# The second expert rows of token block 0 are fetched in the front, by halves

## The chip, the cores and the metric

One NeuronCore of a Trainium2 chip runs the whole program in one launch. The figure of merit is the device time in microseconds. The kernel before takes 3671.69 us, the median of 3 runs (3661.53 to 3674.93). The engines are PE (TensorE, matrix multiply), DVE (VectorE), ACT (ScalarE), POOL (GpSimd, which issues the gathers by index) and SP (SyncE, which issues the plain loads and stores).

## The reference, cut to what matters

There are 1024 tokens of 1024 features, in 8 blocks of 128 tokens. A mixing part (latent attention with rotary positions, a gated linear recurrence, a merge) gives `h2`. Then comes an expert layer, in float32:

```python
s = einsum('thpd,hpnd->thpn', (xt @ w_query).reshape(...), sub_keys)   # 8 heads, 2 halves, 128 keys
s_top, i_top = top_k(s, 16); best, pos = top_k(cand, 16)               # 16 of 16384 experts per head
u = expert_u[idx]; v = expert_v[idx]                                   # 128 rows of 1024 per token, each
act = gelu(einsum('td,thkd->thk', xt, u))
x  += gate2 * einsum('thk,thkd->td', softmax(best) * act, v)
```

So each token needs 128 "first rows" of `expert_u` (dot products) and 128 "second rows" of `expert_v` (a weighted sum). Both tables hold 16384 rows of 4 KB, 67 MB each.

## The kernel before

**Front.** The tokens go through the mixing part in two halves of 512 (p = 0 and p = 1): attention, the gate of branch A with its projection (`merge_a`), the recurrence (`lru`), the gate of branch B with its projection (`merge_b`), the output projection (`ffn_in`, tiles `ps_z`) and the expert query (`ps_qr`, `ps_sc`) with its top 16. A float32 product is made of three passes over a high and a low part (lines 686, 687, 689).

**Last stage (`dense`, from about 1656 us).** Blocks 1, 2, 3 and 4 are not gathered. PE goes through all 128 groups of 128 experts: it multiplies the group's `expert_u` with these 512 tokens (`ps_A`, 24 matmuls), weighs the result with a table of chosen experts (`Gt`, read from `d_G`) and multiplies with the group's `expert_v` (`ps_y`, 96 matmuls for each four groups). Both tables are read once, in order, by SP (`raw<-in_uT`, `raw<-in_expert_v`), 512 KB each.

**Gathered blocks.** Blocks 0, 5, 6 and 7 fetch their rows by index. For the first rows POOL issues one indirect DMA for each of the 128 choices: 128 tokens, 4 KB each (`g_u`), and DVE makes the dot product (lines 1120 and 1140). For the second rows POOL fetches, token by token, that token's 128 rows (`g_v`, line 1160), and PE sums them: the weights stand in one column of a zero tile of 32 columns, four tokens side by side in the four column groups of PE (`g_y`, line 1174, two passes for each float32 product). The expert numbers are `ei`, their transpose `eT`, the weights `wT`.

**What sets the order.** Beside the main program there is a list of small steps. `pump(n)` takes the next n steps from it at many places of the main program; `self.rate` says how many (attention unit, weight matrix `w`, `z`, `q`). In the second half of the front the list holds block 0's first rows, three choices a step through three buffers (43 steps), spread evenly (`merge`) among the steps that build the tables of the dense blocks 1 to 3 (`differ`, `keys`, `product`, `leave`: tiles `ps_d`, `oneA`, `oneB`, `ps_G`, `gs`). What is left is done before the last stage begins. In `dense` the list is paced evenly: `points = (128 + 32*4) * RATE` (248 with `RATE` 0.97) and `rate = len(steps) / points`, one point for each 24 matmuls. Before, that list has 959 steps: 131 gathers of first rows each for blocks 5, 6, 7 and 128 of second rows each for blocks 0, 5, 6, 7, with some steps around them, and the routing of 6 and 7. The two kinds are merged with each other:

```python
self.steps += self.merge(us[5][:48], routes) + self.merge(us[5][48:], vs[0][:80]) + \
    self.merge(us[6], vs[0][80:] + vs[5][:64]) + self.merge(us[7], vs[5][64:] + vs[6][:64]) + \
    vs[6][64:] + vs[7]
```

A scheduler then sets the order on each engine; each engine takes its instructions in that order, and one that waits holds up all behind it. Front tiles come from pools in SBUF (tags `t2`, `t4`, `gu`, ...) and from 8 PSUM banks (`ps`).

Of the kernel before, what the change touches and what calls it, by code (L numbers as in the profile page):

```python
# [9 lines left out]
F32 = mybir.dt.float32  # L10
F32R = mybir.dt.float32r
I32 = mybir.dt.int32
# [19 lines left out]
GUF = 3  # L32
# [52 lines left out]
class Builder:  # L85
    def __init__(self, ctx, tc, I, out, dbg=None, stop=None):
# [8 lines left out]
        self.rate = dict(unit=(1, 1.6), w=(1.5, 2.2), z=(4, 5), q=(2, 2.5))  # L95
# [149 lines left out]
    def prep(self, ap):  # L245
# [34 lines left out]
        nc.sync.dma_start(gr[:, 1, :], I["k_norm_g"][None, 64:96].to_broadcast([128, 32]))  # L280
        for w in range(2):
            g1 = gr[:, w, None, 0:16].to_broadcast([128, 8, 16])
            g2 = gr[:, w, None, 16:32].to_broadcast([128, 8, 16])
            nc.vector.tensor_tensor(self.tab[:, 2 * w, :, 0:16], cn, g1, op=ALU.mult)
            nc.vector.tensor_tensor(self.tab[:, 2 * w, :, 16:32], sn, g2, op=ALU.mult)
            nc.vector.tensor_tensor(self.tab[:, 2 * w + 1, :, 0:16], sn, g1, op=ALU.mult)
            nc.vector.tensor_tensor(self.tab[:, 2 * w + 1, :, 16:32], cn, g2, op=ALU.mult)
# [91 lines left out]
    def head(self, p):  # L379
# [6 lines left out]
        def load():  # L386
            s["x"] = []
            for i in range(4):
# [277 lines left out]
    def rope(self, dst, src, which, tb, n):  # L666

        nc = self.nc
        t1 = self.tab[:, 2 * which, tb, None, :].rearrange("p o (a b) -> p o a b", a=2).to_broadcast([128, n, 2, 16])
        t2 = self.tab[:, 2 * which + 1, tb, None, :].rearrange("p o (a b) -> p o a b", a=2).to_broadcast([128, n, 2, 16])  # L670
# [286 lines left out]
    def route(self, tb):  # L957
# [83 lines left out]
        def end():  # L1041
# [6 lines left out]
            if tb in GATHER:  # L1048
# [4 lines left out]
                g["eT"] = self.kept(g, [128, 128], I32, "eT")  # L1053
# [8 lines left out]
        def turn():  # L1062
# [3 lines left out]
            nc.vector.tensor_copy(g["eT"], pt)  # L1066
# [8 lines left out]
    def kept(self, g, shape, dt, name):  # L1075

        tb = g["tb"]
        return self.cp.tile(shape, dt, name=f"{name}{tb}") if tb in SOONER or name == "eT" and tb == BRIDGE else \
# [6 lines left out]
    def after_part(self, p):  # L1085
# [5 lines left out]
        if p == 0:  # L1091
            self.steps += rt[0] + self.merge(self.gather_u(self.blocks[0]), dense)
# [55 lines left out]
    def gather_v(self, g):  # L1148
# [30 lines left out]
        return [lambda n=n: step(n) for n in range(128 + GV - 4)] + [lambda: self.finish(gp, g["tb"], g.pop("y"), "gv", GV)]  # L1179

# [206 lines left out]
    def run(self):  # L1387
# [5 lines left out]
        self.d_hT = [dr.tile([128, 4, 512], F32, name=f"d_hT{j}") for j in range(4)]  # L1393
        self.d_v = dr.tile([128, 4, 512], F32, name="d_v")
# [6 lines left out]
        with (tc.tile_pool(name="front_b", bufs=1, reuse_waits="tile") as fb,  # L1401
              tc.tile_pool(name="front_a", bufs=9, reuse_waits="tile") as fa,
              tc.tile_pool(name="ps", bufs=8, space=bass.MemoryType.PSUM, reuse_waits="tile") as self.ps):
            self.fp = Pair(fa, fb, ("b8", "whl", "raw"))
            self.tab = self.fp.tile([128, 4, 8, 32], F32, tag="tab", bufs=1, name="tab")
# [77 lines left out]
```

## Time and profile before

| | |
|---|---|
| median of 3 runs | 3671.69 us |
| the profiled execution | 3655.58 us |
| its span, first to last instruction | 3653.8 us |
| front (to the first `ps_A` matmul) | about 1656 us |
| last stage | about 1998 us |
| PE, DVE, POOL, ACT busy | 87%, 63%, 34%, 33% of the span |
| DMA | 915 MB moved, 250 GB/s over the span |

The profile is one execution. Busy time of an engine says how long instructions ran on it; a wait is idle time before an instruction, put down to what released it. `PEclk` is the clock that PE was granted, as a share of the full 2.4 GHz. The DMA share is the mean busy share of the 16 DMA engines.

### The profile page before, as it was taken

How to read it: one execution, taken by the hardware profiler on the slowest of the kernel's cores; microseconds unless marked ns; L12 is line 12 of the kernel's file. 1: busy time of each engine (PE TensorE's matmuls, PEld its weight loads, DVE VectorE, ACT ScalarE, POOL GpSimd, SP SyncE). 2: the span in 40 equal slices, each digit the busy share in tenths (PEclk: the TensorE clock that was granted, in tenths of full speed). 3: DMA queues.
4: the chain of work that ended last, by engine and by line, in shares of the span. 5: the costliest groups of instructions: out<-in, count | busy, mean ns of one | idle time of the engine just before them, and what ended most of it. 6: DMA issues, size and time to landing. Idle time of an engine off the chain costs nothing.

```text
span 3653.8 us, 42970 instructions
## 1 busy us (share of the span) xinstructions
PE 3189.4 (87%) x15408; PEld 2341.4 (64%) x15408; DVE 2305.6 (63%) x5350; ACT 1189.6 (33%) x1861; POOL 1243.4 (34%) x1052
## 2 busy tenths in 40 slices
PE   6899989599987988867798988898988989899997
PEld 4477778467765776645565665665666666666665
DVE  5535557988788567696965655665646665633334
ACT  4437444376356333233221121121211221212121
POOL 0000013133332000002456645554746655544451
PEclk8899999799998999878999999998999999999999
DMA  8422444166866433228899989898989999999995
GB/s 313 151 85 88 136 152 146 51 200 223 289 209 209 144 116 120 72 110 268 266 338 354 369 309 332 329 346 289 372 307 348 367 338 345 335 345 338 356 362 192
DMA packets 388990, 915.13 MB, mean 250 GB/s; under 512 B 160020, under 2 KB 178068, under 8 KB 384936
## 3 DMA queue, kind: packets, MB, share of 16 engines
q0 software_dynamic: 147456, 536.94, 39.9%
q1 hardware_dynamic: 241320, 375.45, 31.2%
q8 instruction: 121, 1.98, 0.2%
q14 instruction: 93, 0.76, 0.1%
HBM read 851.44 MB, written 60.83 MB: 250 GB/s over the span
## 4 chain that ended last, share of the span: by engine, by line
PE 29%; DMA 28%; DVE 21%; issue 14%; ACT 5%; POOL 3%; SPq 0%; POOLq 0%; DVEq 0%; ACTq 0%
DMA raw<-in_uT 13%; DMA raw<-in_expert_v 6%; DMA g_u<-in_expert_u,g_ei 5%; DVE g_u L1120 3%; PE g_y L1174 2%; DMA g_u<-in_expert_u,ei 2%; PE ps_y L686 2%; DVE v L105 2%; PE ps_G L1238 2%; PE ps_y L687 2%; DVE yac L1347 1%; PE ps_y L689 1%; POOL g_u L1132 1%; DVE u L105 1%; ACT u L104 1%
## 5 line engine op out<-in xcount | busy, mean ns | idle before, releaser
L1120 DVE CUSTOM_DVE_ANT_0 g_u<-g_u,g_h 128x1024 f32<-128x1024 f32 x384 | 462.2, 1220 | 140.8 <-DMA g_u<-in_expert_u,g_ei 81.1
L686 PE MATMUL ps_A<-dh,u 128*128 128x512 f32 x1024 | 443.3, 433 | 117.5 <-ACT u L104 100.9
L686 PE MATMUL ps_y<-v,w 128*128 128x512 f32 x1024 | 419.0, 409 | 60.4 <-DVE yac L1347 37.3
L105 DVE TENSOR_TENSOR u<-raw,u 128x1024 fp32r<-128x1024 f32 x128 | 156.7, 1224 | 448.9 <-ACT u L104 413.7
L687 PE MATMUL ps_A<-dh,u 128*128 128x512 f32 x1024 | 430.1, 420 | 7.9 <-DMA dh<-d_h2T 7.9
L1114 POOL DMA_INDIRECT g_u<-in_expert_u,g_ei x256 | 312.7, 1221 | 331.9 <-DVE g_act L1120 145.4
L687 PE MATMUL ps_y<-v,w 128*128 128x512 f32 x1024 | 408.7, 399 | 0.0
L104 ACT CAST u<-raw 128x1024 fp32r<-128x1024 f32 x128 | 133.9, 1046 | 806.5 <-DMA raw<-in_uT 731.4
L1114 POOL DMA_INDIRECT g_u<-in_expert_u,ei x128 | 163.9, 1281 | 646.6 <-DVE ei L1057 440.8
L686 PEld LDWEIGHTS ps_A<-dh,u 128*128 128x128 f32 x1024 | 212.7, 208 | 230.1 <-ACT u L104 124.5
L1160 POOL DMA_INDIRECT g_v<-in_expert_v,eT x256 | 302.5, 1182 | 121.1 <-issue 71.3
L1160 POOL DMA_INDIRECT g_v<-in_expert_v,g_eT x256 | 261.5, 1022 | 231.1 <-PE g_y L1174 132.3
L686 PEld LDWEIGHTS ps_y<-v,w 128*128 128x128 f32 x1024 | 197.1, 192 | 162.7 <-issue 46.9
L1132 POOL DMA_INDIRECT g_u<-in_expert_u,g_ei x128 | 151.7, 1185 | 397.2 <-DVE g_act L1140 184.1
L104 ACT CAST v<-raw 128x1024 fp32r<-128x1024 f32 x128 | 134.2, 1048 | 463.7 <-DMA raw<-in_expert_v 224.2
L689 PE MATMUL ps_y<-v,w 128*128 128x512 f32 x1024 | 279.4, 394 | 0.0
L1174 PE MATMUL g_y<-g_v,g_z 128*32 128x512 f32 x2048 | 259.6, 599 | 11.5 <-DMA g_v<-in_expert_v,eT 11.1
L689 PE MATMUL ps_A<-dh,u 128*128 128x512 f32 x1024 | 253.4, 389 | 2.1 <-DVE u L105 2.1
L687 PEld LDWEIGHTS ps_A<-dh,u 128*128 128x128 f32 x1024 | 211.7, 207 | 53.8 <-DMA dh<-d_h2T 8.9
L105 POOL TENSOR_TENSOR whl<-wraw,whl 128x1024 fp32r<-128x1024 f32 x16 | 40.6, 2544 | 586.7 <-ACT whl L104 586.7
L105 DVE TENSOR_TENSOR whl<-wraw,whl 128x1024 fp32r<-128x1024 f32 (+2 forms) x136 | 155.5, 1145 | 129.5 <-ACT whl L104 129.4
L105 DVE TENSOR_TENSOR v<-raw,v 128x1024 fp32r<-128x1024 f32 x128 | 156.5, 1223 | 125.8 <-ACT v L104 113.7
(370 smaller groups left out, 6555.8 us busy)
## 6 DMA issues: line engine op xcount, KB each, us to landing
raw<-in_uT SPq DMA_DIRECT2D x128, 512.0 KB
raw<-in_expert_v SPq DMA_DIRECT2D x128, 512.0 KB
wraw<-in_w_in SPq DMA_DIRECT2D x64, 512.0 KB
d_G<-gs SPq DMA_DIRECT2D x64, 512.0 KB
Gt<-d_G SPq DMA_DIRECT2D x32, 1024.0 KB
wada<-in_w_ada SPq DMA_DIRECT2D x32, 512.0 KB
wraw<-in_w_query SPq DMA_DIRECT2D x32, 512.0 KB
x<-in_x SPq DMA_DIRECT2D x16, 512.0 KB
```

The costliest lines, as they stand in the source:

```text
L104: self.nc.scalar.copy(hi, src)
L105: (eng or self.nc.vector).tensor_tensor(lo, src, b32(hi), op=ALU.subtract)
L686: nc.tensor.matmul(ps, lh, rh, start=(n == 0), stop=False)
L687: nc.tensor.matmul(ps, lh, rl, start=False, stop=False)
L689: st = nc.tensor.matmul(ps, ll, rh, start=False, stop=(n == len(terms) - 1))
L1114: st = nc.gpsimd.indirect_dma_start(out=u[:], out_offset=None, in_=I["expert_u"], in_offset=bass.IndirectOffsetOnAxis(ap=g["ei"][:, s:s + ...
L1120: nc.vector.tensor_tensor_reduce(out=u, in0=u, in1=g["h2"], scale=1.0, scalar=0.0, op0=ALU.mult, op1=ALU.add, accum_out=g["act"][:, s:s + 1])
L1132: fetch = lambda s: [nc.gpsimd.indirect_dma_start(out=us.setdefault(k, gp.tile([128, 1024], F32, tag="gu", bufs=GUN, name="g_u"))[:], out_ ...
L1160: st = nc.gpsimd.indirect_dma_start(out=v[:], out_offset=None, in_=I["expert_v"], in_offset=bass.IndirectOffsetOnAxis(ap=g["eT"][:, t:t + ...
L1174: nc.tensor.matmul(g["y"][q * 32:(q + 1) * 32, hf * 512:(hf + 1) * 512], zs[n // 16][:, q, (r % 4) * 32:(r % 4 + 1) * 32], v4[q][:, hf * 5 ...
L1238: nc.tensor.matmul(ps[:, m, :], B[:, m, :], A[:, m, :], start=True, stop=True)
L1347: nc.vector.tensor_tensor(yac[tb][:, ds], yac[tb][:, ds], ps, op=ALU.add)
```

## The change

Block 0's second rows move from the last stage to the front, behind its first rows in the same list (`sooner_v`, new). 128 tokens are not fetched as 128 rows of 4 KB each, but for each half of the 1024 columns as 128 rows of 2 KB: 256 indirect DMAs in place of 128. A step n has four tokens of one half: PE sums step n-1 (four matmuls), then POOL issues step n into two tiles of two tokens. The tiles are the three of `gu` and the one of `gh`, so two steps fit. At the end of each half (n = 32 and 64) the result is scaled, added and stored (`close`). There are 65 such steps; the rates of the second half rise so that the longer list is done in the same program. The sums have a PSUM bank of their own (`py`), so `ps` in the front has 7 banks. The rotary table, 16 KB per partition, is split: one half of it in SBUF, the other in DRAM (`d_tab`) until the second half of the front reads it. In the last stage the list has 866 steps: no second rows of block 0, 40 empty steps beside block 5's first rows, and then blocks 6 and 5, 7 and 6 paired.

```diff
-        self.rate = dict(unit=(1, 1.6), w=(1.5, 2.2), z=(4, 5), q=(2, 2.5))
+        self.rate = dict(unit=(1, 2), w=(1.5, 2.9), z=(4, 6.6), q=(2, 3.3))
...
+        tab = self.fp.tile([128, 4, 8, 32], F32, tag="t4", bufs=8, name="tabs")
...
+        nc.scalar.copy(self.tabs[0], tab[:, :, 0:4, :])
+        nc.sync.dma_start(self.d_tab, tab[:, :, 4:8, :])
...
+            if p:
+                self.tabs.append(fp.tile([128, 4, 4, 32], F32, tag="tab", bufs=1, name="tab"))
+                nc.sync.dma_start(self.tabs[1], self.d_tab)
...
+            if tb in SOONER:
+                g["eh"] = [self.fp.tile([128, 128], I32, tag="g_eh", bufs=2, name="g_eh") for _ in range(2)]
+                for hf in range(2):
+                    nc.vector.tensor_scalar(g["eh"][hf], pt, 2.0, float(hf), op0=ALU.mult, op1=ALU.add)
...
-            self.steps += rt[0] + self.merge(self.gather_u(self.blocks[0]), dense)
+            self.steps += rt[0] + self.merge(self.gather_u(self.blocks[0]) + self.sooner_v(self.blocks[0]), dense)
...
+    def sooner_v(self, g):
+        halves = I["expert_v"].rearrange("e (h c) -> (e h) c", h=2)
+        def rows(n):
+            hf, r = divmod(n, 32)
+            for k in range(2):
+                tag, bufs = ("gh", 1) if (2 * n + k) % (GUF + 1) == GUF else ("gu", GUF)
+                v = fp.tile([128, 2, 512], F32, tag=tag, bufs=bufs, name="h_v")
+                for m in range(2):
+                    tok = (2 * k + m) * 32 + r
+                    nc.gpsimd.indirect_dma_start(out=v[:, m, :], out_offset=None, in_=halves,
+                        in_offset=bass.IndirectOffsetOnAxis(ap=g["eh"][hf][:, tok:tok + 1], axis=0))
+            z = t["z", n] = fp.tile([128, 4, 32], F32, tag="hz", bufs=2, name="h_z")
+            nc.vector.memset(z, 0.0)
+            nc.vector.tensor_copy(z[:, :, r:r + 1], g["wT"][:, :, r:r + 1])
+        def sums(n):
+            for q in range(4):
+                nc.tensor.matmul(t["y"][q * 32:(q + 1) * 32, :], z[:, q, :], v[q // 2][:, q % 2, :],
+                                 start=(r == 0), stop=(r == 31), tile_position=(0, q * 32))
...
+        def step(n):
+            if n and n <= 64:
+                sums(n - 1)
+                if n % 32 == 0:
+                    close(n // 32 - 1)
+            if n < 64:
+                rows(n)
...
-              tc.tile_pool(name="ps", bufs=8, space=bass.MemoryType.PSUM, reuse_waits="tile") as self.ps):
+              tc.tile_pool(name="py", bufs=1, space=bass.MemoryType.PSUM, reuse_waits="tile") as self.py,
+              tc.tile_pool(name="ps", bufs=7, space=bass.MemoryType.PSUM, reuse_waits="tile") as self.ps):
...
+            idle = [lambda: None]
+            self.steps += self.merge(us[5], routes + idle * 40) + self.merge(us[6], vs[5]) + self.merge(us[7], vs[6]) + vs[7]
```

On POOL, after block 0's 128 first rows, the order was this, with the last stage's gathers of both kinds from the 45th on (`ei` and `eT` belong to blocks 5 and 0 there):

```order
L1132 DMA g_u<-in_expert_u,g_ei 128x1024 x128
L1114 DMA g_u<-in_expert_u,ei_13442 128x1024 x44
L1160 DMA g_v<-in_expert_v,eT_6123 128x1024
L1114 DMA g_u<-in_expert_u,ei_13442 128x1024 x2
L1160 DMA g_v<-in_expert_v,eT_6123 128x1024
L1114 DMA g_u<-in_expert_u,ei_13442 128x1024 x3
```

With the change POOL has, between the front's first rows and the last stage:

```order
L1146 DMA g_u<-in_expert_u,g_ei 128x1024 x128
L1209 DMA h_v<-in_expert_v,g_eh 128x512 x256
L1128 DMA g_u<-in_expert_u,ei_14301 128x1024 x128
L1174 DMA g_v<-in_expert_v,eT_14302 128x1024
L1128 DMA g_u<-in_expert_u,g_ei 128x1024
```

All 256 half-row gathers stand ahead of the last stage's first gather, and block 5's first rows have no second rows among them.

On PE in `merge_b`, between the end of a gate product (`ps_gb`) and the next projection (`ps_pb`), there stood two steps of the table building:

```order
L689 MATMUL ps_gb<-hT,whl 128x512 x8
L1238 MATMUL ps_G<-oneA,oneB 128x128 x4
L1220 LDWEIGHTS first
L1220 MATMUL ps_d<-idb,first 128x512
L1222 LDWEIGHTS ones
L1222 MATMUL ps_d<-ones 128x512
...
L1222 MATMUL ps_d<-ones 128x512
L686 MATMUL ps_pb<-rec,whl 128x512
```

Now there is one step of the tables at such a place and two of block 0's sums (`h_y`, four matmuls each):

```order
L695 MATMUL ps_gb<-hT,whl 128x512 x8
L1222 MATMUL h_y<-h_v,h_z 32x512 x4
L1302 MATMUL ps_G<-oneA,oneB 128x128 x4
L1284 LDWEIGHTS first
L1284 MATMUL ps_d<-idb,first 128x512
L1286 LDWEIGHTS ones
L1286 MATMUL ps_d<-ones 128x512
L1222 MATMUL h_y<-h_v,h_z 32x512 x4
L692 MATMUL ps_pb<-rec,whl 128x512
```

Each `h_y` group stands in front of a product of the main program, which cannot begin until those rows have landed. Counted over PE's whole order, of the 256 `h_y` matmuls 60 stand in `lru` (from the first `ps_g` to the first `ps_pb`), 71 in `merge_b` (to the first `ps_z`), 62 in the output projection (to the first `ps_qr`) and 63 in the query; the number of `ps_G` matmuls in each of these differs from before by at most four.

On PE at the seam between `merge_b` and the output projection, before:

```order
L689 MATMUL ps_pb<-rec,whl 128x512 x8
L109 MATMUL ps_z<-whl,yT 128x256
L110 MATMUL ps_z<-whl,yT 128x256
L111 MATMUL ps_z<-whl,yT 128x256
```

and with the change:

```order
L695 MATMUL ps_pb<-rec,whl 128x512 x8
L1222 MATMUL h_y<-h_v,h_z 32x512 x3
L109 MATMUL ps_z<-whl,yT 128x256
L1222 MATMUL h_y<-h_v,h_z 32x512
L110 MATMUL ps_z<-whl,yT 128x256
L111 MATMUL ps_z<-whl,yT 128x256
```

The four matmuls of one step are placed singly here, one between the three passes of a product. On DVE, between the first and the last row maximum of the second half's attention (`mx`), 45 dot products of block 0 stood before and 63 stand now; the rest of the 128 follow up to the first quarter of `lru`, in place of up to the start of `merge_b`.

## Rows read from the trace of the kernel before

**Rows 1.** Busy time by stage of the front's second half; columns in line one.
```profile
core 0: us, PE busy (x) PEld busy (x) DVE busy (x) ACT busy (x) POOL busy (x), PEclk, DMA share, GB/s
640.00:890.00 250.00, 202.92 (x1134) 152.04 (x1132) 226.80 (x882) 148.75 (x319) 63.89 (x52) 0.88 0.48 157
1000.00:1162.00 162.00, 128.48 (x525) 95.36 (x526) 136.91 (x275) 90.03 (x117) 47.42 (x38) 0.89 0.60 201
1162.00:1295.00 133.00, 127.94 (x612) 99.01 (x611) 84.05 (x122) 65.75 (x98) 11.80 (x9) 0.97 0.50 170
1295.00:1356.00 61.00, 55.23 (x418) 51.31 (x416) 36.51 (x61) 12.47 (x17) 0.00 (x0) 0.94 0.27 87
1356.00:1560.00 204.00, 167.11 (x823) 130.60 (x822) 148.14 (x626) 71.90 (x126) 0.00 (x0) 0.89 0.29 103
```

**Rows 2.** The last stage in four stretches, same columns.
```profile
1656.00:2200.00 544.00, 464.11 (x2018) 340.09 (x2019) 370.79 (x683) 128.18 (x162) 282.42 (x233) 0.92 0.92 323
2200.00:3200.00 1000.00, 873.65 (x3976) 623.06 (x3979) 607.79 (x917) 202.50 (x258) 567.64 (x471) 0.94 0.94 337
3200.00:3600.00 400.00, 395.67 (x2059) 256.06 (x2052) 141.16 (x185) 79.96 (x102) 189.69 (x192) 1.00 0.96 341
3600.00:3654.00 54.00, 34.40 (x151) 27.83 (x149) 22.56 (x25) 6.39 (x9) 0.00 (x0) 0.84 0.41 146
```

**Rows 3.** VectorE adds of line 1347 in three of them: us, busy (xcount).
```profile
1656.00:2200.00 544.00, 37.21 (x56) 0.92 0.92 323
2200.00:3200.00 1000.00, 84.61 (x128) 0.94 0.94 337
3200.00:3600.00 400.00, 36.67 (x56) 1.00 0.96 341
```

**Rows 4.** Waits, last stage: engine line <- releaser: us in total, times, longest.
```profile
ACT u L104 <- DMA raw<-in_uT: 731.4, 104, 30.6
```

**Rows 5.** Waits of PE in the last stage, same columns.
```profile
PE ps_A L686 <- ACT u L104: 100.9, 36, 9.7
```

**Rows 6.** PE in order of time: start us, us, instruction.
```profile
3377.71 0.39 PE L686 MATMUL ps_A<-dh,u 128*128 128x512 f32 x1
3377.94 0.39 PE L687 MATMUL ps_A<-dh,u 128*128 128x512 f32 x1
...
3380.52 2.28 PE L1174 MATMUL g_y<-g_v,g_z 128*32 128x512 f32 x16
3382.74 0.50 PE L686 MATMUL ps_y<-v,w 128*128 128x512 f32 x1
```

**Rows 7.** Costliest groups: line, instruction | busy us, mean ns | idle before.
```profile
L1132 POOL DMA_INDIRECT g_u<-in_expert_u,g_ei x128 | 151.7, 1185 | 397.2 <-DVE g_act L1140 184.1
```

**Rows 8.** DMA queues: packets, MB, share of 16 engines.
```profile
q0 software_dynamic: 147456, 536.94, 39.9%
```

**Rows 9.** POOL in order of time, one gather of the front.
```profile
1022.84 1.68 POOL L1132 DMA_INDIRECT g_u<-in_expert_u,g_ei  x1 [2.35 <-DVE g_act L1140]
```

**Rows 10.** VectorE in order of time, the dot product on those rows.
```profile
1028.94 1.22 DVE L1140 CUSTOM_DVE_ANT_0 g_u<-g_u,g_h 128x1024 f32<-128x1024 f32 x1 [1.99 <-DMA g_u<-in_expert_u,g_ei]
```

**Rows 11.** Waits of VectorE in the front, columns as before.
```profile
DVE g_u L1140 <- DMA g_u<-in_expert_u,g_ei: 64.5, 41, 4.6
```

**Rows 12.** Line 1132, the front's gathers: ns min/median/max, first and last start.
```profile
L1132 POOL DMA_INDIRECT g_u<-in_expert_u,g_ei x128: 935/941/2585, 728.4 to 1209.9; - x128
```

**Rows 13.** Line 1140, their dot products, same columns.
```profile
L1140 DVE CUSTOM_DVE_ANT_0 g_u<-g_u,g_h x128: 1174/1219/1274, 733.9 to 1220.6; 128x1024 f32<-128x1024 f32 x128
L1140 DVE DVE_READ_ACCUMULATOR2_ANT g_act<- x128: 71/82/93, 735.0 to 1221.8; 128x1 f32 x128
```

**Rows 14.** Lines 1165, 1166: padded weights of the last stage, same columns.
```profile
L1165 DVE MEMSET g_z<- x32: 485/485/485, 1830.0 to 3550.3; 128x512 f32 x32
L1166 DVE COPY g_z<-g_wT x24: 165/182/189, 2389.3 to 3550.8; 128x16 f32<-128x16 f32 x24
```

**Rows 15.** Waits of PE in the front.
```profile
PE ps_G L1238 <- DVE oneA L1231: 56.8, 14, 11.1
```

More of the change, by code (lines that the diff above doesn't have):

```diff
@@ L668, in rope @@
         nc = self.nc
-        t1 = self.tab[:, 2 * which, tb, None, :].rearrange("p o (a b) -> p o a b", a=2).to_broadcast([128, n, 2, 16])
-        t2 = self.tab[:, 2 * which + 1, tb, None, :].rearrange("p o (a b) -> p o a b", a=2).to_broadcast([128, n, 2, 16])
+        t1 = self.tabs[tb // 4][:, 2 * which, tb % 4, None, :].rearrange("p o (a b) -> p o a b", a=2).to_broadcast([128, n, 2, 16])
+        t2 = self.tabs[tb // 4][:, 2 * which + 1, tb % 4, None, :].rearrange("p o (a b) -> p o a b", a=2).to_broadcast([128, n, 2, 16])
         ab = self.fp.tile([128, 2, n, 2, 16], F32, tag="t2", name="rope")
@@ L1052, in end @@
                         (self.gp if late else self.fp).tile([128, 128], dt, tag="g_" + n, bufs=1, name="g_" + n)
-                g["eT"] = self.kept(g, [128, 128], I32, "eT")
+                if tb not in SOONER:
+                    g["eT"] = self.kept(g, [128, 128], I32, "eT")
                 nc.vector.tensor_copy(g["w"], W2)
@@ L1077, in kept @@
         tb = g["tb"]
-        return self.cp.tile(shape, dt, name=f"{name}{tb}") if tb in SOONER or name == "eT" and tb == BRIDGE else \
+        if tb in SOONER:
+            return self.fp.tile(shape, dt, tag="g_" + name, bufs=1, name="g_" + name)
+        return self.cp.tile(shape, dt, name=f"{name}{tb}") if name == "eT" and tb == BRIDGE else \
             self.gp.tile(shape, dt, tag="g_" + name, bufs=3 if name == "wT" else 2, name="g_" + name)
@@ L1393, in run @@
         self.d_hT = [dr.tile([128, 4, 512], F32, name=f"d_hT{j}") for j in range(4)]
+        self.d_tab = dr.tile([128, 4, 4, 32], F32, name="d_tab")
         self.d_v = dr.tile([128, 4, 512], F32, name="d_v")
@@ L1421, in run @@
             us = {tb: self.gather_u(self.blocks[tb]) for tb in GATHER if tb not in SOONER}
-            vs = {tb: self.gather_v(self.blocks[tb]) for tb in GATHER}
-            self.steps += self.merge(us[5][:48], routes) + self.merge(us[5][48:], vs[0][:80]) + \
-                self.merge(us[6], vs[0][80:] + vs[5][:64]) + self.merge(us[7], vs[5][64:] + vs[6][:64]) + \
-                vs[6][64:] + vs[7]
+            vs = {tb: self.gather_v(self.blocks[tb]) for tb in GATHER if tb not in SOONER}
+            idle = [lambda: None]
+            self.steps += self.merge(us[5], routes + idle * 40) + self.merge(us[6], vs[5]) + self.merge(us[7], vs[6]) + vs[7]
             self.dense(da, db)
```

32 lines of the change are left out of this document (26 added, 6 removed).

## The prediction

> **What bounds the kernel now.** I read the table of busy time by stage first, then the waits, then single stretches in order of time. In the front's second half no engine is the bound throughout [rows 1]. In attention (640 to 890 us) DVE is busy 227 of 250 us. In the recurrence (1000 to 1162) DVE is busy 137 and PE 128 of 162 us. In `merge_b` (1162 to 1295) PE is busy 128 of 133 us, in the output projection (1295 to 1356) 55 of 61, in the query (1356 to 1560) 167 of 204. The DMA engines are 27 to 60% busy from 1000 us on, and POOL is hardly busy after 1162 us [rows 1].
>
> The last stage is another machine. From 2200 to 3200 us the DMA engines are 94% busy at 337 GB/s, PE only 87% at a granted clock of 0.94, a mean of its two levels of 1.2 and 2.4 GHz [rows 2]. The longest wait is ACT's for the table `raw<-in_uT`, 731 us in all, and 101 us of it comes through to PE [rows 4, 5]. So the middle is bound by transfers. In the last 400 us PE is 99% busy as well as DMA 96% [rows 2]: both bind.
>
> The pace there is set by points of 24 matmuls, so I turn it into time per point. Half the points belong to `ps_y`, each with two adds of line 1347 (the first group's eight are copies by ACT). The 128 adds of the middle [rows 3] are 64 such points, 128 points in all: 1000 / 128 = 7.81 us. The late stretch has 56 adds, 56 points: 400 / 56 = 7.14 us. The first has 56 adds and 8 copies, 64 points: 544 / 64 = 8.5 us. PE alone would need 0.23 us from matmul to matmul, 24 x 0.23 = 5.5 us a point, and 2.22 us for 16 passes of `g_y`, which are four gathers: 0.555 us a gather [rows 6].
>
> **The last stage after the change.** The list has 866 steps in place of 959, over 248 points: 3.49 a point in place of 3.87. Three phases follow from the code. (a) Block 5 beside routing and empty steps, 201 steps, 57.6 points: 128 gathers are 2.2 a point, 2.2 x 0.524 MB, and 0.656 MB of tables (168 MB over 256 points), 1.82 MB. At 337 GB/s that is 5.4 us, and PE needs 5.5. The ends are 5.5 and the 8.5 of the first stretch; both limits meet there and the start is in it, so I take the middle, 7.0: 403 us. (b) Two pairs of blocks, 532 steps, 152.4 points with 3.36 gathers: 2.42 MB, 7.2 us at 337 GB/s (PE would need 5.5 + 1.68 x 0.555 = 6.4; unchanged would be 7.81): 1097 us. (c) The last block's second rows, 133 steps, 38.1 points, like the late stretch at 7.14: 272 us. The end stays at 54. Sum 1826 against 1998: **-172 us**.
>
> Two other ways bound it. The queue of gathers took 39.9% of 16 engines for 147456 packets [rows 8]: 0.399 x 16 x 3653.8 / 147456 = 158 ns each; 16384 fewer are 162 us of the 16 engines, and at a share of 0.94 also 172 us. By bytes it is 67.1 MB at 334 GB/s, 201 us, the upper end. The lower end is PE's work alone: 64 groups at 1.11 us, 71 us.
>
> **What the front pays.** A `h_y` group of four matmuls is eight passes, 1.11 us by [rows 6], 71 us in all. Where they stand I take from the order. In `merge_b` 71 matmuls, 17.75 groups, on an engine that has 5 us free: +20. In the projection 15.5 groups are 17 us beside 55 of 61; POOL must issue 62 half rows there at 1.185 us [rows 7], 73 us, so this stretch becomes about 80: +19. In recurrence and query 30.75 groups, 34 us, beside 34 and 37 us of idle PE; part of that idle time has a cause that does not move (57 us in the front for `oneA` [rows 15]), so half: +17. In attention DVE gets 18 more dot products of 1.22 + 0.08 us [rows 13], 23 us on a full engine; they leave the recurrence, where DVE is busy 85%: +8.
>
> Then there is the wait itself. The half rows were not in any trace. One step's four gathers cost POOL 4 x 1.185 = 4.7 us; at their fastest, 0.935 [rows 12], 3.7. A gather issued from 1022.84 to 1024.52 let its dot product start at 1028.94 [rows 9, 10]: 4.4 us to land. A step is asked for two steps ahead, so 9.1 us against two steps of some 8 us each (500 us for 64). On average it is there in time; where two groups stand together it is not. The nearest row is the same fetch of first rows, scheduled in the same way: 64.5 us in 41 waits over 43 batches [rows 11], 1.5 us a batch. The ends for 64 steps are 0 and 96 us; I take the middle, 48. What stands behind a waiting `h_y` is the main program's next product, so this time is not hidden.
>
> The rest: 64 zero tiles and 64 copies on DVE, at most 0.485 and 0.18 us [rows 14], lie beside DVE's idle time there; two closings, one table store and load, one copy on ACT, and 7 PSUM banks for 8 I put at 5 us, with 0 and 25 as ends. On SP the closings' stores wait for DVE with weight loads behind them, twice, which is in those 5. Sum: 20 + 19 + 17 + 8 + 48 + 5 = **+117 us**.
>
> The Trainium skill speaks against this part (SBUF — State Buffer, Who interferes with whom): a float32 copy of DVE within SBUF can lock GpSimd out of the port through which it writes the descriptors of its gathers. By that rule the 64 fills (if they count like copies) and copies hold POOL up by at most 64 x 0.665 = 43 us, 0.7 us a step; the projection would then need 15.5 x 5.4 = 84 us and the sum would be 4 us more. In this trace an issue takes 0.94 us in the median and up to 2.59 [rows 12], which does not say what made the long ones long.
>
> **Sum.** -172 + 117 = -55 us. The profiled execution took 3655.6 us (span 3653.8), 16 us under the median of 3671.7. Its own sum is 3600.6; against the median it is **3617 us**.
>
> **Rivals.** (1) The front hides it. PE and DMA idle most where the sums go, and a PE with fewer gaps is granted a higher clock (0.89 in the recurrence, 0.97 in `merge_b` [rows 1]). Then only `merge_b` and the projection pay, 39 us, and the last stage gains its 201: 3510 us. Against it: a queue in fixed order fills gaps only if the rows have landed. (2) The transfer taken out was hidden anyway. PE is 99% busy at the end of the run [rows 2]; if it binds everywhere once DMA eases, the last stage gains PE's 71 us and the front still pays 117: 3718 us. Against it are the 101 us in which PE waits for tables [rows 5]. The same case would follow from the skill (HBM Reference, Specifications (TRN2)), where a core that streams alone gets about 425 GB/s rather than a share of 358: with 425 DMA would have room. The middle's 337 at a busy share of 0.94 come to 358, so the trace speaks for a full queue. (3) Slower: PE stands at the half rows. Two steps in flight need (4.7 + 4.4 + 1.1) / 2 = 5.1 us each; if PE has to sit through that, it pays 64 x 5.1 = 327 us less the 82 us that PE idles from 1000 to 1560 now, +245 against -172: 3745 us. Without waits the front pays 69, so 103 us are left for them: the change loses from 1.6 us of wait a step on, just above the 1.5 that the first rows show. (4) That the sums slip behind the front is excluded by the order: the last `h_y` stands in the query.
>
> **How the numbers follow.** Forecast 0.52, with its own range 3565 to 3680; rival 1 0.22; rival 2 0.10; rival 3 0.12; 0.04 for none of them. A change under 0.5% (18 us) can't be told from none here. Faster by more: 0.43 of the forecast, all of rival 1, 0.02 of rival 2, together 0.67. Within: 0.07 of the forecast, 0.03 of rival 2, 0.03 of the rest, 0.13. Slower: 0.02 of the forecast, 0.05 of rival 2, all of rival 3, 0.01 of the rest, 0.20. The range for 8 in 10 goes from rival 1 to rival 2, 3505 to 3715.
>
> **What would show it.** Right: the first `ps_A` about 117 us later than 1656; 1097 us for the paired blocks at a DMA share still near 0.94; waits of PE for `h_v` of 30 to 70 us. A front under 50 us longer is rival 1. A last stage with PE over 97% busy and DMA clearly under 0.9, gaining about 71 us, is rival 2. Waits of PE for `h_v` over 103 us are rival 3. The forecast is wrong as a mechanism if the time per point of the paired blocks stays at 7.8 us.

## The result, and the profile of the changed kernel

The changed kernel takes 3611.24 us, the median of 3 runs (3608.46 to 3616.83), against 3671.69: a ratio of 0.9844, 95% interval 0.9809 to 0.9880. Forecast were 3617 us. Its profiled execution took 3616.83 us, the slowest of the three, while that of before was 16 us under its median, so stages of the two traces are compared as lengths, and the sizes of effects are taken from ratios. A stage begins here with the first product of its name:

| stage (first product) | before, us | changed, us | difference | predicted |
|---|---|---|---|---|
| attention and `merge_a` (up to `ps_g` 1002.7, 1055.9) | | | +53 | +8 |
| recurrence (`ps_g` to `ps_pb`) | 188.2 | 194.1 | +6 | +17 with the query |
| `merge_b` (to `ps_z`) | 102.4 | 128.3 | +26 | +20 |
| output projection (to its last product) | 61.1 | 84.9 | +24 | +19 |
| query (to the last `ps_qr`) | 200.3 | 199.6 | -1 | see recurrence |
| tail (to `ps_A`) | 101.8 | 97.4 | -4 | 0 |
| front together (`ps_A` at 1656.5, 1760.2) | | | +104 | +117, 53 of it for waits and small parts |
| last stage | 1997 | 1855 | -142 | -172 |

The busy time by stage, which answers to [rows 1] (columns in the first line; attention, `merge_a`, recurrence, `merge_b`, projection, query, tail):

```profile
core 0: us, PE busy (x) PEld busy (x) DVE busy (x) ACT busy (x) POOL busy (x), PEclk, DMA share, GB/s
640.00:937.00 297.00, 229.68 (x1237) 166.77 (x1238) 257.76 (x918) 160.95 (x336) 95.52 (x76) 0.87 0.53 174
937.00:1056.00 119.00, 98.81 (x431) 74.30 (x430) 84.32 (x137) 35.05 (x56) 47.77 (x40) 0.90 0.79 268
1056.00:1250.00 194.00, 169.22 (x756) 111.99 (x755) 150.88 (x390) 113.38 (x148) 92.25 (x80) 0.96 0.66 217
1250.00:1378.00 128.00, 125.93 (x635) 82.78 (x634) 57.84 (x110) 40.98 (x65) 73.64 (x73) 1.00 0.78 258
1378.00:1463.00 85.00, 77.32 (x501) 55.30 (x499) 39.44 (x83) 12.06 (x16) 49.47 (x44) 0.96 0.63 197
1463.00:1665.00 202.00, 187.01 (x988) 126.26 (x987) 154.69 (x657) 72.69 (x123) 78.43 (x77) 0.97 0.63 210
1665.00:1760.00 95.00, 60.86 (x341) 40.50 (x339) 86.22 (x281) 35.84 (x72) 0.94 (x1) 0.80 0.31 114
```

The idle DMA share of the front is filled (0.63 to 0.78 where there was 0.27 to 0.60), and PE in the projection has now 8 idle microseconds of 85. The tail is untouched: DVE is busy 86 of 95 us there, PE 61.

The last stage, which answers to [rows 2], same columns, and its waits, which answer to [rows 4, 5] (us in total, times, longest):

```profile
1760.00:2200.00 440.00, 370.63 (x1508) 296.79 (x1509) 346.87 (x645) 115.63 (x147) 177.62 (x142) 0.92 0.88 285
2200.00:3200.00 1000.00, 916.46 (x4252) 657.97 (x4251) 615.72 (x918) 215.51 (x274) 555.55 (x471) 0.96 0.95 339
3200.00:3550.00 350.00, 344.24 (x1728) 230.21 (x1727) 144.30 (x196) 75.70 (x97) 163.03 (x155) 1.00 0.93 329
3550.00:3615.00 65.00, 44.57 (x202) 34.82 (x201) 29.11 (x32) 8.90 (x12) 0.00 (x0) 0.86 0.40 130
```
```profile
ACT u L104 <- DMA raw<-in_uT: 620.3, 106, 22.0
PE ps_A L692 <- ACT u L104: 89.7, 35, 7.6
```

The middle still runs at a DMA share of 0.95 and 339 GB/s; only the work per point is less.

A point is 24 matmuls, of `ps_A` or of `ps_y`. [rows 3] counted the adds behind `ps_y` instead. But the program multiplies five groups with the tokens (`ps_A`) before the first `ps_y`, so at the start a count of adds falls behind the points, and at the end it catches up. Counted by matmuls, first `ps_A`, then `ps_y`, the changed kernel from its first `ps_A` to 57.6, to 210 and to 248 points (us, PE busy and count, clock, DMA share, GB/s):

```profile
1760.00:2164.00 404.00, 184.51 (x711) 0.92 0.87 280
2164.00:3270.00 1106.00, 455.40 (x1834) 0.96 0.95 338
3270.00:3548.00 278.00, 108.46 (x456) 1.00 0.95 335
```
```profile
1760.00:2164.00 404.00, 156.82 (x672) 0.92 0.87 280
2164.00:3270.00 1106.00, 442.32 (x1824) 0.96 0.95 338
3270.00:3548.00 278.00, 108.66 (x454) 1.00 0.95 335
```

The first phase takes 404 us, 7.0 us a point (forecast 403). POOL agrees: its first gather of a second row, which opens the pairs, starts at 2167.0 us, 407 us behind the first `ps_A`. The paired blocks take 1106 us, 7.26 a point (forecast 1097 and 7.2), the last rows 278 us, 7.3 a point (forecast 272 and 7.14), the end 67 us (54).

The first and the late stretch of the kernel before by the same count, again `ps_A`, then `ps_y`:

```profile
1656.00:2200.00 544.00, 235.44 (x888) 0.92 0.92 323
3200.00:3600.00 400.00, 142.47 (x595) 1.00 0.96 341
```
```profile
1656.00:2200.00 544.00, 186.51 (x775) 0.92 0.92 323
3200.00:3600.00 400.00, 160.97 (x672) 1.00 0.96 341
```

The first stretch holds 1663 / 24 = 69.3 points, 7.85 us each, where the adds said 64 and 8.5. The late one holds 52.8 points, 7.58 us each, where they said 56 and 7.14. The middle stays at 7.8.

### The profile page after: what moved, and what is told of

It reads as the page before. It is cut to its first block, busy times and chain, and to the rows that moved or that the text cites. A ratio compares the mean times of both kernels' runs of the same rounds, so it can differ in the third digit from the quotient of the medians.

```text
span 3615.1 us, 43218 instructions
## 1 busy us (share of the span) xinstructions
PE 3196.5 (88%) x15408; PEld 2320.3 (64%) x15408; DVE 2326.8 (64%) x5465; ACT 1192.0 (33%) x1860; POOL 1375.2 (38%) x1180
## 3 DMA queue, kind: packets, MB, share of 16 engines
q0 software_dynamic: 149504, 536.94, 41.9%
## 4 chain that ended last, share of the span: by engine, by line
PE 37%; DMA 25%; DVE 19%; issue 11%; ACT 4%; POOL 3%; another core or an unknown queue 0%; SPq 0%; DVEq 0%; POOLq 0%; ACTq 0%
DMA raw<-in_uT 9%; DMA g_u<-in_expert_u,g_ei 5%; DMA raw<-in_expert_v 4%; DVE g_u L1134 3%; PE ps_G L1302 2%; PE ps_y L692 2%; DMA g_u<-in_expert_u,ei 2%; PE ps_y L695 2%; PE g_y L1188 2%; PE ps_y L693 2%; PE h_y L1222 2%; DVE v L105 2%; POOL g_u L1146 2%; PE ps_A L692 1%; PE ps_A L693 1%
## 5 line engine op out<-in xcount | busy, mean ns | idle before, releaser
L692 PE MATMUL ps_A<-dh,u 128*128 128x512 f32 x1024 | 433.3, 423 | 100.6 <-ACT u L104 89.7
L693 PE MATMUL ps_A<-dh,u 128*128 128x512 f32 x1024 | 422.7, 413 | 8.0 <-DMA dh<-d_h2T 8.0
L1128 POOL DMA_INDIRECT g_u<-in_expert_u,g_ei x256 | 298.6, 1167 | 309.3 <-issue 100.8
L1174 POOL DMA_INDIRECT g_v<-in_expert_v,g_eT x256 | 284.8, 1112 | 255.0 <-PE g_y L1188 101.4
L1209 POOL DMA_INDIRECT h_v<-in_expert_v,g_eh x256 | 273.6, 1069 | 283.1 <-PE h_y L1222 212.8
L692 PEld LDWEIGHTS ps_A<-dh,u 128*128 128x128 f32 x1024 | 206.9, 202 | 198.0 <-ACT u L104 110.9
L692 PEld LDWEIGHTS ps_y<-v,w 128*128 128x128 f32 x1024 | 195.2, 191 | 124.4 <-issue 36.9
L1146 POOL DMA_INDIRECT g_u<-in_expert_u,g_ei x128 | 152.6, 1192 | 282.4 <-DVE g_act L1154 116.3
L695 PE MATMUL ps_A<-dh,u 128*128 128x512 f32 x1024 | 253.1, 389 | 0.8 <-DVE u L105 0.8
L104 ACT CAST whl<-wraw 128x1024 fp32r<-128x1024 f32 (+2 forms) x152 | 151.1, 995 | 297.1 <-PE ps_pb L695 55.2
L693 PEld LDWEIGHTS ps_A<-dh,u 128*128 128x128 f32 x1024 | 206.9, 202 | 52.8 <-DMA dh<-d_h2T 9.0
L695 PEld LDWEIGHTS ps_y<-v,w 128*128 128x128 f32 x1024 | 194.6, 190 | 46.3 <-DVE w L105 4.0
```

The costliest lines, as they stand in the source:

```text
L104: self.nc.scalar.copy(hi, src)
L692: nc.tensor.matmul(ps, lh, rh, start=(n == 0), stop=False)
L693: nc.tensor.matmul(ps, lh, rl, start=False, stop=False)
L695: st = nc.tensor.matmul(ps, ll, rh, start=False, stop=(n == len(terms) - 1))
L1128: st = nc.gpsimd.indirect_dma_start(out=u[:], out_offset=None, in_=I["expert_u"], in_offset=bass.IndirectOffsetOnAxis(ap=g["ei"][:, s:s + ...
L1146: fetch = lambda s: [nc.gpsimd.indirect_dma_start(out=us.setdefault(k, gp.tile([128, 1024], F32, tag="gu", bufs=GUN, name="g_u"))[:], out_ ...
```

## The experiments

All ratios are to the kernel before, with a 95% interval; 0.001 is 3.7 us. The interval of one ratio is 7 to 15 us to either side, so differences between two of them of under some 20 us are not shown by them alone. Stages of two traces differ without a change of the code too: the front of the kernel before, unchanged, took 1656 us in its own trace and 1671 in that of the next run, and the last stage took 1828 to 1855 us in the ten traces that have the changed kernel's list there.

**The last stage without any second rows of block 0.** The front is before's, the list of the last stage the changed one.

```diff
-            vs = {tb: self.gather_v(self.blocks[tb]) for tb in GATHER}
...
+            vs = {tb: self.gather_v(self.blocks[tb]) for tb in GATHER if tb not in SOONER}
+            idle = [lambda: None]
+            self.steps += self.merge(us[5], routes + idle * 40) + self.merge(us[6], vs[5]) + self.merge(us[7], vs[6]) + vs[7]
```

> The front of before, untouched (8 banks, its rates), and the last stage's list of the changed kernel: block 0's second rows are fetched and summed nowhere, so its output rows are left out. This is the last stage's gain by itself. My theory: the middle of the last stage is bound by transfers, the gain there is what the changed kernel's trace shows, 140 to 172 us: 3500 to 3530 us. The rival that these transfers were hidden anyway says PE's work alone, 71 us: about 3600 us.

Measured: 3515.42 us, 0.9573 (0.9533 to 0.9613). The last stage by itself gains 157 us, and what the changed kernel does in its front costs 0.9844 - 0.9573 = 0.0271, 99 us. That the transfer was hidden anyway falls. The run takes the rows out and pairs the blocks anew at once; the new pairing alone was not run.

**Seven PSUM banks in the front of the kernel before.**

```diff
-              tc.tile_pool(name="ps", bufs=8, space=bass.MemoryType.PSUM, reuse_waits="tile") as self.ps):
+              tc.tile_pool(name="ps", bufs=7, space=bass.MemoryType.PSUM, reuse_waits="tile") as self.ps):
```

> The kernel before with 7 PSUM banks in the front in place of 8, nothing else. In the changed kernel attention and merge_a of the second half together took 53 us longer, where I had 8. Theory: that is the dot products of the first rows, squeezed into these stages (110 in place of 80); then 7 banks cost 0 to 10 us: 3672 to 3682 us. Rival: the missing bank delays the softmax of attention; then these stages are some 40 us longer here too: about 3710 us.

Measured: 3646.97 us, 0.9952 (0.9933 to 0.9972). The bank is no cost; with seven the kernel before is even some 18 us faster, which neither side expected. It shortens several stages by little (`ps_pb` starts 7 us earlier, `ps_A` 5), and its cause stays open.

**The sums without the fetch.** The changed kernel, but rows are fetched for the first step alone and all 64 sums read them.

```diff
             for k in range(2):
+                if n:
+                    vs.setdefault(n, []).append(t["v", k])
+                    continue
...
```

> The changed kernel with the half rows of the first step fetched only and read again by all 64 steps: PE's sums without transfers, without POOL's issues and without waits for them (block 0's sums are of other rows). Theory (the front pays mostly PE's own work, waits are some 30 us of it): 20 to 50 us less than the changed kernel, 3560 to 3590. Rival (the fetch and its waits are the main price): 80 us less or more, under 3530.

Measured: 3543.58 us, 0.9666 (0.9635 to 0.9697), between the two. The fetch with its waits is 0.9844 - 0.9666 = 0.0178, 65 us; the sums, the packing of the first rows and what else the front has changed (seven banks among it) are 0.0093, 34 us. Both have an interval of almost 20 us to either side.

**The fetch without the sums.** All 256 half rows are fetched, but PE sums only the first and the last step of each half.

```diff
-            for q in range(4):
+            for q in range(4 if r in (0, 31) else 0):
```

> The changed kernel with all 256 gathers, but PE sums only the first and the last step of each half, 4 of 64 steps (the other sums are left out). Theory (PE's work in stages where PE is full is the price): merge_b and the output projection come back to about their old length, 45 to 60 us less than the changed kernel: 3550 to 3565. Rival (the transfers are the price): less than 20 us gained, 3590 or more.

Measured: 3684.63 us, 1.0049 (1.0023 to 1.0074), slower than before, against both. PE's order held the sums of the last step of a half far too early, so that PE stood through the fetch. The waits of line 1222 (us in total, times, longest), and the issues of the half rows (ns min/median/max, first and last start; below it POOL's idle time by what ended it):

```profile
PE h_y L1222 <- DMA h_v<-in_expert_v,g_eh: 162.2, 2, 87.3
```
```profile
L1209 POOL DMA_INDIRECT h_v<-in_expert_v,g_eh x256: 941/949/5519, 1093.8 to 1553.0; - x128
...
  DMA h_v<-in_expert_v,g_eh: 87.1, 57
  issue: 66.9, 195
```

As a measure of the fetch's price the run is void. But it shows two things. With nearly nothing on PE to wait for, 256 issues still take 459 us, 7.2 us a step: 4 x 0.95, some 0.3 between two, and waits for rows to land. And PE standing in the front for that long makes the change a loss, as rival 3 had it in kind.

**The packing alone.** The kernel before, its second rows where they were, with block 0's first rows packed into the first 43 of 108 places at the changed rates.

```diff
-        self.rate = dict(unit=(1, 1.6), w=(1.5, 2.2), z=(4, 5), q=(2, 2.5))
+        self.rate = dict(unit=(1, 2), w=(1.5, 2.9), z=(4, 6.6), q=(2, 3.3))
...
-            self.steps += rt[0] + self.merge(self.gather_u(self.blocks[0]), dense)
+            self.steps += rt[0] + self.merge(self.gather_u(self.blocks[0]) + [lambda: None] * 65, dense)
```

> The kernel before with nothing moved to the front, but block 0's first rows packed into the first 43 of 108 places of the front's list (65 empty steps behind them) at the changed kernel's rates, as the changed kernel packs them. The sums alone, with the packing, cost 0.9666 - 0.9573 = 0.0093, 34 us of front over no second rows at all, and there attention and merge_a were 48 us longer. Theory (the packing is what costs: dot products on a DVE that is full in attention, which later stages give back only in part): 20 to 45 us slower than before, 3688 to 3715 against 3668. Rival (the sums cost the 34 us, the packing is given back in recurrence, projection and query): within 10 us of before, 3658 to 3678.

Measured: 3655.35 us, 0.9979 (0.9955 to 1.0003). The rival holds: the packing costs nothing, since what attention and `merge_a` pay (`ps_g` starts at 1048.8 against 1002.7) the recurrence (179 us for 188) and the query (172 for 202) give back. So the sums alone are 0.9666 - 0.9573 + 0.0021 = 0.0114, 42 us, with some 20 to either side; the fronts of the two traces differ by 38. This run has eight PSUM banks and the run of the sums seven: if the 18 us of the run with seven banks add up with the rest, the sums cost 60. `merge_b` and the projection, first with the packing alone, then with packing and sums (columns as in the first fence):

```profile
1228.00:1329.00 101.00, 100.61 (x492) 79.49 (x491) 53.86 (x73) 40.13 (x64) 0.00 (x0) 1.00 0.39 134
1329.00:1393.00 64.00, 57.67 (x420) 54.02 (x419) 36.63 (x61) 12.36 (x16) 0.00 (x0) 0.92 0.26 85
```
```profile
1235.00:1356.00 121.00, 121.00 (x639) 82.27 (x639) 58.17 (x113) 41.05 (x65) 0.00 (x0) 1.00 0.35 120
1356.00:1424.00 68.00, 67.94 (x496) 52.01 (x495) 38.14 (x82) 11.23 (x15) 0.00 (x0) 1.00 0.24 78
```

On a full PE (`merge_b`) the sums cost all of their time, 20 us; in the projection some 4, since PE had gaps, and without them its granted clock is 1.00 for 0.92. The changed kernel needs 128 and 85 us there: the fetch adds another 7 and 16 or 17.

**Whole rows.** The changed kernel with 128 indirect DMAs of 4 KB rows in place of 256 of 2 KB: two tokens a step, both column halves side by side in the one bank.

```diff
-            hf, r = divmod(n, 32)
-            for k in range(2):
...
+            k, r = divmod(n, 32)
+            for m in range(2):
+                tag, bufs = ("gh", 1) if (2 * n + m) % (GUF + 1) == GUF else ("gu", GUF)
+                v = fp.tile([128, 1024], F32, tag=tag, bufs=bufs, name="h_v")
+                vs.setdefault(n, []).append(v)
+                tok = (2 * k + m) * 32 + r
+                nc.gpsimd.indirect_dma_start(
+                    out=v[:], out_offset=None, in_=I["expert_v"],
+                    in_offset=bass.IndirectOffsetOnAxis(ap=g["eh"][:, tok:tok + 1], axis=0))
...
```

> The changed kernel with the second rows of block 0 fetched as whole rows of 4 KB: 128 indirect DMAs in place of 256, two tokens a step, four matmuls a step as before, both column halves side by side in the one PSUM bank, each bank closed after 64 tokens. The same bytes, the same matmuls, the same places in the list, the same four tiles. Theory A (POOL's issues set the pace of the fetch: 0.95 + 0.30 us each, four a step, 5.0 of the 7.2 us a step seen without sums): two issues a step are 3.0 us, most of the 65 us that the fetch cost go, 30 to 55 us faster than the changed kernel, 3555 to 3582. Theory B (the rows' landing and the DMA engines set it, the bytes are the same): within 12 us of the changed kernel, 3600 to 3623.

Measured: 3586.87 us, 0.9785 (0.9744 to 0.9825): 22 us under the changed kernel, between A and B, and the intervals touch. Its first `ps_A` stands at 1742.7, 17.5 us earlier; its projection takes 73 us for 85, its recurrence 186 for 194. The issues and POOL's idle time, whole rows first, then the changed kernel:

```profile
L1206 POOL DMA_INDIRECT h_v<-in_expert_v,g_eh x128: 935/941/3760, 1095.4 to 1626.0; - x128
...
  PE h_y L1221: 365.2, 55
```
```profile
L1209 POOL DMA_INDIRECT h_v<-in_expert_v,g_eh x256: 940/946/2728, 1096.5 to 1651.7; - x128
...
  PE h_y L1222: 212.8, 42
  issue: 60.0, 195
```

An issue takes the same time for a row of 4 KB as for one of 2 KB, so half of them takes half the time. With whole rows POOL waits for PE's free tiles most of the time. So the issues look like a part of the fetch's price, about a third, not most of it. This is argued and not shown alone: 22 us have some 20 to either side, the zero tiles are half as large here, and the queue of gathers was busy some 20 us less too (41.6% of 3592.0 us for 41.9% of 3615.1).

**Lower rates.** The changed kernel with all four rates a tenth lower, so that 11 of the 64 steps stand behind the query.

```diff
-        self.rate = dict(unit=(1, 2), w=(1.5, 2.9), z=(4, 6.6), q=(2, 3.3))
+        self.rate = dict(unit=(1, 1.8), w=(1.5, 2.6), z=(4, 5.9), q=(2, 3))
```

> The changed kernel with the four rates of the second half a tenth lower (1.8, 2.6, 5.9, 3 for 2, 2.9, 6.6, 3.3), so that the last 11 of the 64 steps stand behind the last product of the query, where only DVE's choice of the 16 best runs on (1665 to 1760 us in the changed kernel, PE 64% busy). Theory (a wait of PE for half rows costs nothing in a stretch that DVE bounds, and attention gets fewer dot products): 11 steps at 1 us of sums and 1 us of wait and some 5 dot products less, 15 to 35 us faster, 3576 to 3596. Rival (the tail only moves the end of the front, since the list must be empty before the last stage begins, and PE's main products then end no earlier): 3605 to 3640.

Measured: 3591.51 us, 0.9814 (0.9779 to 0.9849): by the ratio 11 us under the changed kernel, which this run alone does not separate from nothing.

**Whole rows and lower rates.** Both edits above.

> Whole rows of 4 KB (128 indirect DMAs, as in e6) and the rates a tenth lower (11 steps behind the query's last product, as in e7) in one kernel. Theory (issues and place are two separate costs): the gains over the changed kernel add, 0.0059 + 0.0030, so 0.9755 of before, some 3577 us. Rival (lower rates helped only because POOL then had more time for its issues, and with half of the issues that gain is gone): 0.978 to 0.980, 3586 to 3594.

Measured: 3558.91 us, 0.9739 (0.9706 to 0.9772). The gains add, and the interval lies clear of the changed kernel's: 38 us faster than it, 96 faster than before. Against whole rows alone, the last product of the query ends 63 us earlier, 29 of them already up to `ps_g`, and the tail is 36 us longer.

**Three zero tiles.** The changed kernel with one more buffer for `h_z`.

```diff
-            z = t["z", n] = fp.tile([128, 4, 32], F32, tag="hz", bufs=2, name="h_z")
+            z = t["z", n] = fp.tile([128, 4, 32], F32, tag="hz", bufs=3, name="h_z")
```

> The changed kernel with three buffers for the zero tile h_z in place of two, nothing else. DVE waited 49 us in 16 waits before it could clear a zero tile, until PE had read it two steps earlier (33 us of that even where no rows are fetched), and the weights that DVE splits for PE stand behind. Theory (this wait comes back to PE and is part of what the sums cost): 10 to 30 us faster than the changed kernel, 0.9765 to 0.982. Rival (DVE idles there anyway, the wait only takes the place of another): within 8 us of the changed kernel, 0.982 to 0.9865.

Measured: 3612.52 us, 0.9880 (0.9846 to 0.9914): no gain. But the wait did not go: DVE stood idle 40.0 us in 14 waits before it cleared a zero tile, against 49.0 us in 16 with two tiles. So this does not say what the wait costs; why a third tile leaves it stays open.

**Both edits and six zero tiles; rates lower still.** The kernel of whole rows and lower rates with six `h_z` (they are half as large there), and the same with rates 1.6, 2.4, 5.5, 2.7, so that some 20 steps stand behind the query (158 of the 512 passes in the trace).

> Whole rows, rates a tenth lower, and six zero tiles (they are half as large there) together. If the zero tiles' wait is a cost: 0.968 to 0.973, 3550 to 3568. If it is none: as e8, about 0.9755.

> As e10, with rates lower still (1.6, 2.4, 5.5, 2.7), so that 21 of the 64 steps stand behind the query's last product. Theory (what stands there is hidden beside DVE's choice of the 16 best as long as POOL's pace of about 5 us a step lets 100 us hold 20 steps): 5 to 20 us under e10. Rival (the end of the list then sets the end of the front): 5 to 40 us over e10.

Measured: 3562.33 us, 0.9762 (0.9729 to 0.9794), the same as with two (DVE still waits 23.8 us for the zero tiles, against 32.1); and 3581.00 us, 0.9816 (0.9785 to 0.9847), slower. The tail, from the last product of the query to the first `ps_A`, with 11 steps in it (two zero tiles), then with some 20:

```profile
1580.00:1716.00 136.00, 110.17 (x585) 65.70 (x583) 106.27 (x330) 52.48 (x104) 20.25 (x19) 0.86 0.52 184
```
```profile
1555.00:1725.00 170.00, 147.36 (x786) 78.20 (x784) 123.91 (x366) 65.16 (x130) 38.92 (x37) 0.94 0.65 227
```

The tail was 95 us long. With some 20 steps it is 170 us and PE, not DVE, fills it: the end of the list sets the end of the front, as the rival had it.

**More empty steps in the last stage.** Whole rows and lower rates, with 100 empty steps beside block 5's first rows.

```diff
-            self.steps += self.merge(us[5], routes + idle * 40) + self.merge(us[6], vs[5]) + self.merge(us[7], vs[6]) + vs[7]
+            self.steps += self.merge(us[5], routes + idle * 100) + self.merge(us[6], vs[5]) + self.merge(us[7], vs[6]) + vs[7]
```

> The kernel with whole rows and lower rates (e8, 0.9739 of before) with 100 empty steps beside block 5's first rows in place of 40: the list then has 926 steps, 3.73 a point, and block 5's dot products and the routing spread over 70 points in place of 58. It tests what held phase (a) of the last stage at 7.6 us a point where 7.0 were forecast. Theory (DVE held it: from 1850 to 1950 us of the changed kernel DVE is busy 91% with PE at 80% and DMA at 0.80; fewer dot products a point let the tables go faster there): phase (a) holds some 12 points more in nearly the same time, the pairs pay 0.37 x 0.524 MB a point for it, 10 to 25 us faster than e8, 0.967 to 0.971. Rival (the stage's bytes are its bound and are the same): within 8 us of e8, 0.972 to 0.976.

Measured: 3587.93 us, 0.9815 (0.9772 to 0.9857): 28 us slower than with 40, against both. The adds, first with 100 empty steps, then with 40 (us, DVE busy and count, ACT busy and count of the copies for the first eight, clock, DMA share, GB/s):

```profile
1719.00:2200.00 481.00, 41.74 (x63) 4.58 (x8) 0.93 0.81 261
2200.00:3200.00 1000.00, 84.95 (x129) 0.00 (x0) 0.95 0.95 343
```
```profile
1716.00:2200.00 484.00, 37.88 (x56) 4.57 (x8) 0.92 0.87 287
2200.00:3200.00 1000.00, 92.59 (x140) 0.00 (x0) 0.97 0.97 345
```

The 7.6 us a point that this run was to explain came from the count of adds; by matmuls the phase took 7.0, as forecast. The first phase did become faster, 71 adds and copies for 64 in the same time (72.8 points for 68.5 by matmuls), but its DMA share fell to 0.81, and the gathers that it no longer carries make the pairs slower, 129 adds for 140 from 2200 to 3200 us (by matmuls 7.55 us a point in place of 7.17). In this stage, bound by transfers, DMA time left empty early was paid later. Fewer than 40 empty steps were not run.

## Why the prediction was right, and where not

- **Last stage, -172; -142 between the two traces, -157 by the run without second rows.** The mechanism held: the DMA share stayed at 0.95 and the pairs took 7.26 us a point for a forecast of 7.2. Term by term this trace has 404 us for 403, 1106 for 1097, 278 for 272 and an end of 67 for 54. But two readings behind the forecast were wrong, both by the count of adds. The first stretch of before took 7.85 us a point, not 8.5, so the middle to 5.5 was 6.7, and the first phase would have been 385 us: that 403 came out is luck. The late stretch took 7.58, not 7.14, so the last rows would have been 289 us. The two errors cancel in the sum. The end of 54 was what lay behind 3600 us, where 6.3 points were left and not 8. The rest of the difference lies within what the last stage varies by from trace to trace. The queue of gathers agrees with its own bound: 39.9% of 3653.8 us before less 36.8% of 3520.3 in the run without second rows are 162 us of the 16 engines, as forecast.
- **Bandwidth.** A lone core should get about 425 GB/s by the Trainium skill (HBM Reference, Specifications (TRN2)). The trace disagrees here: 339 GB/s at a share of 0.95, which is a full queue at 357, where before gave 358. This is a mix of gathered rows and table loads; no run here streams plainly.
- **Front, +117; +104 by the traces, 99 by the ratios.** `merge_b` (20 for the sums, 20 measured without the fetch), and the projection (80 us forecast from POOL's issues, 85 measured) came out near. For the projection the reason holds in part: whole rows, with half of the issues, bring it to 73 us, but POOL issued 44 gathers there, not 62, and was busy 49 us of 85.
- **Attention, +8.** As a place it is wrong: +53 there and in `merge_a`. DVE made 110 dot products up to 1056 us where it made 80 up to 1003, and waited more for their rows. The first line is the changed kernel from 640 to 1056 us, the second before from 640 to 1003 (busy us, mean ns, idle before):

```profile
L1154 DVE CUSTOM_DVE_ANT_0 g_u<-g_u,g_h 128x1024 f32<-128x1024 f32 x110 | 133.6, 1221 | 58.8 <-DMA g_u<-in_expert_u,g_ei 56.9 <-issue 1.5
```
```profile
L1140 DVE CUSTOM_DVE_ANT_0 g_u<-g_u,g_h 128x1024 f32<-128x1024 f32 x80 | 97.1, 1217 | 34.1 <-DMA g_u<-in_expert_u,g_ei 34.0
```

  I counted 18 more dot products, in attention alone, where 30 came with `merge_a`, no wait of theirs, and nothing given back but in the recurrence. As a sum it is about right by luck: the packing alone costs -8 us (between -16 and +1), because 30 us come back in the query. Most of these were waits of the table building, of which the prediction said that their cause does not move: PE's waits for `oneA`, 56.8 us in 14 [rows 15], are 29.9 with the packing alone, and 6.8 of them in the query where there were 26.8. With the change (us in total, times, longest):

```profile
PE ps_G L1302 <- DVE oneA L1295: 22.7, 12, 4.5
```

- **Sums, 20 + 17 and a part of the projection's 19.** Measured 42 us, or up to 60 if the seven banks count. Recurrence and query were put at half of 34 us; beside the packing alone, the sums lengthen them by 5 and 7.
- **Waits for the half rows, 48.** The fetch costs 65 us, 1.0 us a step, under the 1.6 from which rival 3 decides. As a wait of PE it is mis-sized: PE's own idle time for `h_v` is 14.5 us in 7 waits, under the 30 to 70 that were named as the sign. With the waits of the weight loads, which PE's time may hide, it is 30.6 (idle time of line 1222: us, times):

```profile
  DMA h_v<-in_expert_v,g_eh: 30.6, 25
```

  The rest is not idle time of this line. Stage by stage, the changed kernel's trace is longer than that of the sums without the fetch by 5 us up to `ps_g`, 10 in the recurrence, 7 in `merge_b`, 16 in the projection and 22 in the query. The waits cluster where projection and query meet, where sums stand side by side with little between. PE and its weight loads in order of time (start, us, instruction; in brackets the idle time ahead):

```profile
1463.60 3.85 PE L1222 MATMUL h_y<-h_v,h_z 128*32 128x512 f32 x16
1465.78 0.14 PEld L1222 LDWEIGHTS h_y<-h_v,h_z 128*32 128x32 f32 x2 [0.64 <-DMA h_v<-in_expert_v,g_eh]
1472.82 6.01 PE L1222 MATMUL h_y<-h_v,h_z 128*32 128x512 f32 x14 [5.37 <-DMA h_v<-in_expert_v,g_eh]
```

  The 16 passes that took 2.28 us in [rows 6] take 3.85 and 14 of them 6.01. The sums of the query's stretch, with the fetch and without it (busy us, mean ns):

```profile
L1222 PE MATMUL h_y<-h_v,h_z 128*32 128x512 f32 x168 | 32.7, 647 | 5.6 <-DMA h_v<-in_expert_v,g_eh 5.4 <-issue 0.3
```
```profile
L1224 PE MATMUL h_y<-h_v,h_z 128*32 128x512 f32 x168 | 23.0, 602 | 0.4 <-DVE h_z L1216 0.4
```

  Where rows are late the sums themselves take longer, 32.7 us for 23.0. Two reasons show. The rows come in one after another, and the weight loads of each product wait for its own: the first 16 passes take 3.85 us at the full clock. And behind the idle time of PE the granted clock falls to 0.50, its lower level of 1.2 GHz: there a pass takes 1061 ns in the median, against 593 over all of line 1222 (us, PE and PEld busy in the sums, clock, DMA share, GB/s; then ns min/median/max):

```profile
1463.00:1470.00 7.00, 3.85 (x16) 0.74 (x16) 1.00 0.90 273
1470.20:1477.00 6.80, 4.18 (x9) 0.91 (x10) 0.50 0.96 348
```
```profile
L1222 PE MATMUL h_y<-h_v,h_z x9: 784/1061/1062, 1472.8 to 1476.7; 128*32 128x512 f32 x9
```
- **POOL.** I had 4.7 us a step for four issues; with the gaps between two it is some 5, and the fetch's own pace 7.2. Whole rows, with half of the issues, take 22 us off.
- **Rivals.** That the front hides it falls (99 us), that the transfer was hidden anyway falls (157 us for 71). That PE stands at the rows is real as a mechanism, and the run with PE's sums too early shows it past its point. What rival 1 says of the clock shows: it rose from 0.89 to 0.96 in the recurrence and to 0.97 in the query, and still the front pays. Of what the Trainium skill says of copies that lock GpSimd out (SBUF — State Buffer, Who interferes with whom) no run here shows anything apart. What stands beside the long issues can be counted in the changed kernel's trace: 389 of its 1152 gather issues took over 1.1 us, and 386 of these ran beside a dot product or a `TENSOR_TENSOR` of DVE, 44 beside a copy, cast or fill; 283 ran beside no instruction of DVE, and none of them took that long. So copies, which the prediction priced, are not what most of the long ones have in common. That DVE is the cause was not tested by a run.

## What to carry to other kernels

Move transfers out of a stage that fills the DMA engines into one that leaves them idle, and price each stage by its own bound: on a full PE the added passes cost all of their time, elsewhere a part. Fetch by index in rows as large as fit, since POOL pays for each issue and not for its bytes, and let as many steps fall behind the last big product as that stretch can hold, no more. Count the instructions that make up a point, not others that follow them: at the start and the end of a stage the two differ.

## What the runs showed of the hardware

- An indirect DMA of 128 rows keeps POOL 0.94 us for 2 KB and for 4 KB rows alike, and 60.0 / 195 to 66.9 / 195, some 0.3 us, lie between two.
- A PE pass of the sums lasts 593 ns in the median and up to 1062 ns; all 19 of the 512 that took over 617 ns lie in, or reach into, stretches with a granted clock of 0.50. Without the fetch none took longer than 617 ns.
- In the changed kernel none of the gather issues that ran with no instruction of DVE beside them took over 1.1 us.
- One PSUM bank fewer in the front made the kernel before 0.9952 of its time; the cause was not found.
